# A hybrid decoder layer on one core: the first query block by token, planes and joins by token halves, memory pairs split earlier, and the last root folded into the last sum

## The chip, the core and the metric

One core of a Trainium2 chip runs the whole layer as one program. The metric is the device time of one execution in microseconds. The engines are TensorE (PE, with its weight loads PEld), VectorE (DVE), ScalarE (ACT), GpSimd (POOL) and SyncE (SP). SP issues nearly all DMAs here, the transposing ones too; its queue takes its entries in their order, and so does every engine.

## What is computed

x is 256 tokens by 2048 features, float32. With all weights float32, the reference does

```
hn = rmsnorm(x);  q, k, v, g_ret, xr, yr, g_a, g_b = split(hn @ w_in)
ret_out = silu(g_ret) * groupnorm(retention(rotary(q), rotary(k), v))     # 8 heads
rnn_out = gelu(yr) * rg_lru(causal_dwconv(xr))
h = x + (sigmoid(g_a) * (ret_out @ w_proj_ret) + sigmoid(g_b) * (rnn_out @ w_proj_rnn)) @ w_mix_out
h = h + cross_attention(rmsnorm(h), rmsnorm(mem)) @ xa_w_o                # 256 memory tokens, 4 heads
h = h + (silu(gate) * val) @ ffn_w_down,  gate, val = split(causal_dwconv(rmsnorm(h) @ w_up))
out = rmsnorm(h) * final_norm_w
```

where the last rmsnorm divides each token by sqrt(mean of its 2048 squares + 1e-6).

## The kernel before

**Products.** PE multiplies in a 32-bit format that drops low bits of the operands, so every operand is split into `hi` (rounded) and `lo` (the rest), and each product is done as hi*hi, lo*hi and hi*lo. All products are issued by `mm` (L214) and keep the program's order on PE. A gemm makes a block of 512 output columns for all 256 tokens. `steps_n` makes it by token: the 128 tokens of a half (`tt`) are the stationary operand, 512 weight columns stream, three products per k and half. `steps_t` makes it by feature, for the first query block only: 128 weight columns are stationary and x, hi beside lo, streams; per k four products of 512 columns with the weights' `hi`, and four of 256 with their `lo`. It needs two accumulators; `joined` (L415) adds the two 256-column halves of each (ACT copy L420, DVE sum L421). There are three accumulators in PSUM.

**Weights.** `chunks` and `prefetch` walk through one list of chunks of up to four k (1 MB). For each chunk SP loads `raw` (L252; three buffers), ACT rounds it to `hi` (L279; the very first on DVE, L277) and DVE subtracts for `lo` (L280), two k at a time, with six buffers for each. Loads and splits run two chunks ahead of PE. `later(n, fn)` puts work into the program n + 1 chunks on. The first two blocks, queries and values, alternate chunk by chunk, with sizes 2, 2, 4, 4, 4 (`EARLY`).

**x and mem by feature.** The activations are gathered in `Pairs`: pair i is two k, loaded as `xt` (L533) and split by `split_cols` (ACT L454, DVE L455). A pair is made when it is first asked for; `steps_n` asks ahead after its first token half: for pairs up to min(16, k0 + 3n)/2 - 1.

**Turning blocks.** A block that the next stage needs by feature is turned by DMA: `turned_rows` scales the accumulator into `rows` (DVE, L410 or L412), `by_dma` copies these into two planes of 16-bit halves (`pl`, ACT, L388), two DMA transposes on SP's queue, one for each half of the tokens, turn them into `pt` (L390), and some chunks later `join` puts the planes together as `f` (ACT, L399). The planes are made one word half at a time, over all tokens, and so is the join.

**Residuals.** `residual` makes the four blocks of the mixer's output (and later of the attention's): each is added to the stream on DVE (`nat`, L855), turned by `by_dma`, and split for the next stage's products (`turn`, L454 and L455); `squares` (L873) sums for the norm. `memory_steps` places the memory's work there: the sums from the first block on, and pairs 0 to 3 from the fourth block on, one after each of its chunks. After these blocks come the key and query gemms of the attention (`key_query`); the key gemm reads the memory's pairs.

**The end.** `last_down` makes the last 512 columns in halves of 256 (c) per 128 tokens (tt): add (L1029), sum of squares (L1031), then the sums of all blocks together (L1036, L1037), mean plus eps (`rsqrt_small`, L513), the power -1/2 on POOL (L515), the scaling on DVE and ACT (L1042, L1046, L1048) and the stores (L1050).

**Order.** Instructions are put on each engine by a scheduler with priorities: normally the program's order, earlier under `tc.high_priority`; products and the sums over x are held in order.

Of the kernel before, what the change touches and what calls it, by code (L numbers as in the profile page):

```python
# [17 lines left out]
P = 128  # L18
D = 2048
# [13 lines left out]
PART_BUFS = 6  # L33
AHEAD = 2
WARM = 8
URGENT = 5
FREE = 300
RG_WAIT = 3
EPS = 1e-6
# [99 lines left out]
def hybrid_layer(  # L139
# [38 lines left out]
    def acc():  # L178
        return pm.tile([P, 2, BW], F32, tag="acc", name=nm("acc"))
# [132 lines left out]
            pass  # L312
        return a

    def steps_t(w, row, st, nk, col):

        accs = [acc(), acc()]
        first = gemms[0] == 0
        phase = 0
        for k0, n, parts in chunks(nk, w, row, col):  # L320
            last = k0 + n >= nk
            tiles = [(kk, j) for j in range(2) for kk in range(n)]
            if first and k0 == 0:
                runs = [[(t, pr, kk, j) for t in (0, 1)] for kk in range(n) for pr in range(2) for j in range(2)]
            elif last:
                runs = [[(t, pr, kk, j) for kk, j in tiles] for pr in range(2) for t in (1 - pr, pr)]
            else:
                runs = [[(t, pr, kk, j) for pr in range(2) for kk, j in tiles] for t in (phase, 1 - phase)]
                phase = 1 - phase
            for i, run in enumerate(runs):  # L330
                for t, pr, kk, j in run:
                    k = k0 + kk
                    sx = st[k // 2][:, k % 2, :]
                    part = parts[kk // KH][t][:, kk % KH, (2 * pr + j) * P : (2 * pr + j + 1) * P]
                    a = accs[pr][:, j, :]
                    if t == 1:
                        a, sx = a[:, S:BW], sx[:, 0:S]
                    mm(
                        a, part, sx, start=k == 0 and t == 0, stop=k == nk - 1 and t == 0, skip_group_check=True
                    )  # L340
                if i + 1 == len(runs) // 2 and not last and not first and isinstance(st, Pairs):
                    st[(k0 + n) // 2 + 1]
            yield accs

    def gemm_t(*args):
        return ended(steps_t(*args))

    def products_n(o, sx, hi, lo, tt, start, stop):
        h = sx[:, tt * P : (tt + 1) * P]
        l = sx[:, S + tt * P : S + (tt + 1) * P]  # L350
        mm(o, h, hi, start=start, stop=False)
        mm(o, l, hi, start=False, stop=False)
        mm(o, h, lo, start=False, stop=stop)

    def steps_n(w, row, st, nk, col):

        a = acc()
        for k0, n, parts in chunks(nk, w, row, col):
            for tt in range(2):
                for kk in range(n):  # L360
                    k = k0 + kk
                    hi, lo = (t[:, kk % KH, :] for t in parts[kk // KH])
                    products_n(a[:, tt, :], st[k // 2][:, k % 2, :], hi, lo, tt, k == 0, k == nk - 1)
                if tt == 0 and isinstance(st, Pairs):
                    st[min(NT, k0 + 3 * n) // 2 - 1]
            yield a

    def gemm_n(*args):
# [11 lines left out]
    def by_dma(rows, then, wait=1):  # L380


        planes = big([P, 2, 2, BW], U16, s="pl")
        turned_ = big([P, 2, 4, S], U16, s="pt")
        words = rows.bitcast(U16).rearrange("p t (n h) -> p h t n", h=2)
        with tc.high_priority(FREE):
            for h in range(2):
                act.copy(planes[:, :, h, :], words[:, h])  # L388
        for tt in range(2):
            sp.dma_start_transpose(  # L390
                out=turned_.rearrange("p h f s -> p (h f) s")[:, :, tt * P : (tt + 1) * P],
                in_=planes[:, tt].rearrange("p h n -> p (h n)"),
            )

        def join():
            f = big([P, 4, S], s="f")
            halves_ = f.bitcast(U16).rearrange("p f (s h) -> p h f s", h=2)
            for h in range(2):
                act.copy(halves_[:, h], turned_[:, h])  # L399
            then(f)  # L400

        later(wait, join)

    def turned_rows(a, r, then, wait=1):
# [6 lines left out]
                else:  # L411
                    dve.tensor_scalar_mul(rows[:, tt, :], a[:, tt, :], r[:, tt : tt + 1])  # L412
        by_dma(rows, then, wait)

    def joined(a, s="j"):  # L415

        c = tmp("c")
        o = tmp(s)
        with tc.high_priority(URGENT):
            act.copy(c, a[:, :, S:BW])  # L420
            dve.tensor_tensor(out=o, in0=a[:, :, 0:S], in1=c, op=ALU.add)  # L421
        return o

    def split_pair(src, scale=None):

# [115 lines left out]
            return list.__getitem__(self, i)  # L541

    xs = Pairs(x_t, p_mix, 1)
    q_steps = steps_t("w_in", 0, xs, NT, O_Q)
    v_steps = steps_n("w_in", 0, xs, NT, O_V)
    for _ in EARLY[1:]:
        next(q_steps)
# [35 lines left out]
        dve.scalar_tensor_tensor(out=sin, in0=sin, scalar=sign, in1=rsb, op0=ALU.mult, op1=ALU.mult)  # L583
        dve.tensor_tensor(out=cos, in0=cos, in1=rsb, op=ALU.mult)

    qjoin = [joined(t, "q") for t in next(q_steps)]
    assert next(q_steps, None) is None
    later(0, tables)


# [84 lines left out]
    for g in range(2):  # L675
        dec = big([P, 4, S], s="dec")
        vs, turned = [], ([], [])
        for b, o in enumerate((O_Q, O_K)):
            if g + b:
                def rotate_both(f, o=turned[b]):  # L680
                    o.append(rotated(f[:, 0:2, :]))
                    later(0, lambda: o.append(rotated(f[:, 2:4, :])))

                turned_rows(gemm_n("w_in", 0, xs, NT, o + g * BW), None, rotate_both, 2 - b)
            if b == 1:
                sp.dma_start(
                    out=dec,
                    in_=consts[:, C_DEC + g * 4 * S : C_DEC + (g + 1) * 4 * S].rearrange("p (h s) -> p h s", s=S),
                )
            v = gemm_n("w_in", 0, xs, NT, O_V + g * 1024 + b * BW) if g + b else ended(v_steps)  # L690
            if g + b == 0:
                turned[0].extend(rotated(q) for q in qjoin)
            vs.append(split_rows(v, rs0))
        qr, kr = turned
        gates = []
        for b in range(2):
            a = gemm_n("w_in", 0, xs, NT, O_G + g * 1024 + b * BW)
            t = big([P, 2, BW], s="gate")
            for tt in range(2):
                act.activation(t[:, tt, :], a[:, tt, :], AF.Tanh, scale=half_rs0[:, tt : tt + 1])  # L700
            dve.scalar_tensor_tensor(out=t, in0=t, scalar=1.0, in1=a, op0=ALU.add, op1=ALU.mult)
            gates.append(t)
        retain(g, qr, kr, vs, dec, gates)
# [173 lines left out]
    def memory_steps(b):  # L877
        if b == 0:
            ss = sums()
            for c in range(4):  # L880
                later(c, lambda c=c: sum_squares(mnat[c], ss, c))
            later(4, lambda: rsms.append(rstd_rows(ss)))
        if b == 3:
            ms.load(2)
            for k2 in range(4):
                later(k2, lambda k2=k2: ms[k2])

    h1s = []
    ss1 = residual("w_mix_out", merged, h1s, p_xa, memory_steps)
# [126 lines left out]
            last_down(b0, hid, n, 3)  # L1016

    def last_down(b0, hid, n, b):
        h = hrow[b]
        accs = [acc(), acc()]  # L1020
        parts = [p for _, _, ps in chunks(n, "ffn_w_down", b0 * BW, b * BW) for p in ps]
        for tt in range(2):
            for c in range(2):
                cs = slice(c * S, (c + 1) * S)
                for k in range(n):
                    hi, lo = (t[:, k % KH, cs] for t in parts[k // KH])
                    products_n(accs[c][:, tt, 0:S], hid[k // 2][:, k % 2, :], hi, lo, tt, k == 0, k == n - 1)
                y = h[:, tt, cs]
                dve.tensor_add(y, y, accs[c][:, tt, 0:S])  # L1029
                junk = tp.tile([P, S], F32, tag="tr", bufs=2, name=nm("junk"))  # L1030
                dve.scalar_tensor_tensor(  # L1031
                    out=junk, in0=y, scalar=1.0, in1=y, op0=ALU.mult, op1=ALU.mult,
                    accum_out=ss3[:, tt, b + c : b + c + 1],
                )
            part = sp_.tile([P, 1], F32, tag="pt3", bufs=2, name=nm("pt3"))
            dve.tensor_reduce(out=part, in_=ss3[:, tt, 0:4], axis=AX.X, op=ALU.add)  # L1036
            dve.tensor_scalar(out=part, in0=part, scalar1=1.0 / D, scalar2=EPS, op0=ALU.mult, op1=ALU.add)  # L1037
            r = rsqrt_small(ss3[:, tt, 4:5], 1, 1.0 / D, part)
            for c in (1, 0, 3, 2):
                y = hrow[c][:, tt, :]  # L1040
                if c == 3:
                    dve.scalar_tensor_tensor(  # L1042
                        out=y, in0=y, scalar=r, in1=wfin[1][:, 1, :], op0=ALU.mult, op1=ALU.mult
                    )
                elif c == 1:
                    dve.tensor_scalar_mul(y, y, r)  # L1046
                else:
                    act.mul(y, y, r)  # L1048
# [65 lines left out]
```

## Time and profile before

| what | value |
|---|---|
| runs | 2009.7, 2010.22, 2010.87 us; median 2010.22 |
| the profiled execution | 2008.91 us, its span 2007.1 |
| granted PE clock | 0.999 |
| DMA | 423.02 MB, 211 GB/s over the span |
| PE busy | 1995.5 us of the span |
| last product's end, last store's issue | about 1999.3 and 2002.9 us |

Lines of a timeline read: start, duration, engine and source line, operation, output<-input, shape, how many; in brackets how long the engine was idle before, and what ended that. Lines of a group read: line, engine, operation, shapes, how many | busy us, mean ns of one | idle us before, with what ended it. Lines of the list of waits read: total us, times, longest. Product starts in the trace are modelled, so the pitch between products is the better measure.

### The profile page before, as it was taken

How to read it: one execution, taken by the hardware profiler on the slowest of the kernel's cores; microseconds unless marked ns; L12 is line 12 of the kernel's file. 1: busy time of each engine (PE TensorE's matmuls, PEld its weight loads, DVE VectorE, ACT ScalarE, POOL GpSimd, SP SyncE). 2: the span in 40 equal slices, each digit the busy share in tenths (PEclk: the TensorE clock that was granted, in tenths of full speed). 3: DMA queues.
4: the chain of work that ended last, by engine and by line, in shares of the span. 5: the costliest groups of instructions: out<-in, count | busy, mean ns of one | idle time of the engine just before them, and what ended most of it. 6: DMA issues, size and time to landing. Idle time of an engine off the chain costs nothing.

```text
span 2007.1 us, 23602 instructions
## 1 busy us (share of the span) xinstructions
PE 1995.5 (99%) x9044; PEld 1661.7 (83%) x9044; DVE 1264.2 (63%) x1563; ACT 1248.7 (62%) x1506; POOL 7.7 (0%) x12
## 2 busy tenths in 40 slices
PE   9999999999999999999999999999999999999998
PEld 8888888888888888887888888888888888888887
DVE  6857757888545555457555555666775576664675
ACT  6546648888444455577666655767763566744763
POOL 0000000000000000000000000000000000000000
PEclk9999999999999999999999999999999999999999
DMA  8655657665555566787666545666565566655663
GB/s 318 237 209 168 237 201 197 225 203 186 218 197 191 192 209 212 255 255 249 198 221 213 180 170 195 222 197 232 195 226 210 199 196 219 224 209 201 209 231 126
DMA packets 189376, 423.02 MB, mean 211 GB/s; under 512 B 131664, under 2 KB 136400, under 8 KB 144208
## 3 DMA queue, kind: packets, MB, share of 16 engines
q1 hardware_dynamic: 188832, 421.00, 61.9%
q8 instruction: 70, 1.15, 0.2%
q10 hardware_dynamic: 432, 0.53, 0.1%
q14 instruction: 42, 0.34, 0.0%
HBM read 388.46 MB, written 2.10 MB: 195 GB/s over the span
## 4 chain that ended last, share of the span: by engine, by line
PE 97%; DMA 1%; issue 1%; DVE 0%; ACT 0%; SPq 0%; POOLq 0%; POOL 0%; DVEq 0%; ACTq 0%
PE acc L214 95%; PE sm L214 3%; DMA raw<-in_wall 0%; DMA pt<-pl 0%; DVE lo L280 0%; SPq L252 0%; DVE s L455 0%; SPq L533 0%; ACT f L399 0%; ACT nat L1048 0%; ACT junk L873 0%; DVE nat L855 0%; ACT pl L388 0%; ACT hi L279 0%; POOLq L1110 0%
## 5 line engine op out<-in xcount | busy, mean ns | idle before, releaser
L214 PE MATMUL acc<-hi,s 128*128 128x512 f32 (+1 forms) x5680 | 1739.0, 388 | 1.6 <-DVE s L455 1.6
L280 DVE TENSOR_TENSOR lo<-raw,hi 128x1024 fp32r<-128x1024 f32 (+1 forms) x714 | 860.2, 1219 | 645.5 <-ACT hi L279 628.6
L214 PEld LDWEIGHTS acc<-hi,s 128*128 128x128 f32 x5680 | 1061.7, 188 | 218.9 <-DVE s L455 2.4
L214 PE MATMUL acc<-lo,s 128*128 128x512 f32 (+1 forms) x2840 | 1099.8, 387 | 0.0
L279 ACT CAST hi<-raw 128x1024 fp32r<-128x1024 f32 (+1 forms) x712 | 733.7, 1048 | 500.2 <-PE acc L214 433.7
L214 PEld LDWEIGHTS acc<-lo,s 128*128 128x128 f32 x2840 | 533.2, 188 | 109.1
L399 ACT COPY f<-pt 128x1024 uint16<-128x1024 uint16 x118 | 151.5, 1348 | 76.4 <-DMA pt<-pl 76.4
L388 ACT COPY pl<-rows 128x1024 uint16<-128x1024 uint16 x90 | 89.7, 1044 | 63.8 <-DVE rows L412 55.9
L412 DVE TENSOR_SCALAR rows<-acc,ro 128x512 f32<-128x512 f32 x68 | 47.7, 742 | 3.2 <-PE acc L214 3.2
L971 DVE SCALAR_TENSOR_TENSOR fv<-f,pf,fv 128x255 f32<-128x255 f32 (+1 forms) x88 | 35.8, 477 | 0.7 <-ACT fv L969 0.7
L971 DVE SCALAR_TENSOR_TENSOR fg<-f,pf,fg 128x255 f32<-128x255 f32 (+1 forms) x88 | 35.6, 477 | 0.0
L455 DVE SCALAR_TENSOR_TENSOR s<-f,pb,s 128x256 fp32r<-128x256 f32 x48 | 20.1, 479 | 4.7 <-ACT s L454 4.7
L969 ACT ACTIVATE fv<-f,pf 128x256 f32<-128x256 f32 x44 | 22.8, 590 | 0.0
L969 ACT ACTIVATE fg<-f,pf 128x256 f32<-128x256 f32 x44 | 22.8, 591 | 0.0
L431 ACT ACTIVATE s<-fo 128x512 fp32r<-128x512 f32 x22 | 13.6, 633 | 14.2 <-DVE fo L991 14.2
L780 DVE SCALAR_TENSOR_TENSOR xr<-f,pa,xr 128x255 f32<-128x255 f32 (+2 forms) x48 | 19.9, 478 | 3.2 <-ACT xr L778 3.2
L388 ACT COPY pl<-nat 128x1024 uint16<-128x1024 uint16 x16 | 15.9, 1042 | 8.6 <-DVE nat L855 8.6
L454 ACT ACTIVATE s<-f,pb 128x256 fp32r<-128x256 f32 x48 | 20.6, 498 | 0.0
L214 PEld LDWEIGHTS sm<-s,s 128*128 128x128 f32 x144 | 18.8, 191 | 0.9
L214 PE MATMUL sm<-s,s 128*128 128x256 f32 (+1 forms) x144 | 18.6, 279 | 0.0
L214 PE MATMUL acc<-s,hi 128*128 128x512 f32 x64 | 16.5, 394 | 0.6 <-ACT hi L279 0.4
L443 ACT ACTIVATE v<-acc,ro 128x512 fp32r<-128x512 f32 x16 | 10.9, 684 | 7.7 <-DVE v L444 7.7
(152 smaller groups left out, 623.3 us busy)
## 6 DMA issues: line engine op xcount, KB each, us to landing
raw<-in_wall SPq DMA_DIRECT2D x352, 1024.0 KB, 4.9
nat<-in_x SPq DMA_DIRECT2D x8, 512.0 KB, 8.8
raw<-in_wall SPq DMA_DIRECT2D x6, 512.0 KB, 8.3
nat<-in_mem SPq DMA_DIRECT2D x4, 512.0 KB, 9.3
xt<-in_mem_t SPq DMA_DIRECT2D x8, 256.0 KB, 4.6
pt<-pl SPq DMA_TRANSPOSE x118, 4.3
xt<-in_x_t SPq DMA_DIRECT2D x7, 256.0 KB, 8.4
out<-nat SPq DMA_DIRECT2D x6, 256.0 KB, 2.8
```

Of the source, the lines that this page charges most:

```text
L214: tc.keep_in_program_order(pe.matmul(*a, **k))
L279: act.copy(hi[:, ds], raw[:, cs, :])
L280: dve.tensor_tensor(out=lo[:, ds], in0=raw[:, cs, :], in1=hi[:, ds].bitcast(F32), op=ALU.subtract)
L388: act.copy(planes[:, :, h, :], words[:, h])
L399: act.copy(halves_[:, h], turned_[:, h])
L412: dve.tensor_scalar_mul(rows[:, tt, :], a[:, tt, :], r[:, tt : tt + 1])
L431: act.mul(t[:, :, 0:S], src, scale)
L454: act.activation(t[:, j, 0:S], src[:, j, :], AF.Identity, scale=wcol(j))
L455: dve.scalar_tensor_tensor(out=t[:, j, S:BW], in0=src[:, j, :], scalar=wcol(j), in1=t[:, j, 0:S].bitcast(F32), op0=ALU.mult, op1=ALU.subtract,
L780: dve.scalar_tensor_tensor(out=y[:, s:S], in0=z[:, 0 : S - s], scalar=p_cw(3 - s, t), in1=y[:, s:S], op0=ALU.mult, op1=ALU.add,)
L969: act.activation(y, z[:, j, :], AF.Identity, scale=pf[:, 2, t : t + 1], bias=pf[:, 3, t : t + 1])
L971: dve.scalar_tensor_tensor(out=y[:, s:S], in0=z[:, j, 0 : S - s], scalar=pf[:, 2 - s, t : t + 1], in1=y[:, s:S], op0=ALU.mult, op1=ALU.add,)
```

## The change

`steps_t` and `joined` are gone. The first query block is made by `steps_n`; in its first chunk the products of the two token halves are interleaved so that those with the weights' `lo` come last for each k. The block is turned by `turned_rows` like all others, its join 3 chunks later, and rotated then. `by_dma` makes planes, and joins, one token half at a time. Memory pairs 0 to 3 are placed from the third block's third chunk on. In `last_down` the last block goes to a tile `last` with one more column, which holds sqrt(sum of the other squares + eps * D), made on POOL while the last products run; the last sum of squares takes that column along, with a factor 1/D, and so gives mean plus eps at once.

```diff
-    def steps_t(w, row, st, nk, col):
...
     def products_n(o, sx, hi, lo, tt, start, stop):
         mm(o, h, hi, start=start, stop=False)
         mm(o, l, hi, start=False, stop=False)
+        yield
         mm(o, h, lo, start=False, stop=stop)
+        yield
...
     def steps_n(w, row, st, nk, col):
         a = acc()
+        first = gemms[0] == 0
         for k0, n, parts in chunks(nk, w, row, col):
-            for tt in range(2):
+            if first and k0 == 0:
                 for kk in range(n):
-                    products_n(a[:, tt, :], st[k // 2][:, k % 2, :], hi, lo, tt, k == 0, k == nk - 1)
-                if tt == 0 and isinstance(st, Pairs):
-                    st[min(NT, k0 + 3 * n) // 2 - 1]
+                    for _ in zip(*(tile_(tt, kk) for tt in range(2))):
+                        pass
+            else:
+                for tt in range(2):
+                    for kk in range(n):
+                        for _ in tile_(tt, kk):
+                            pass
+                    if tt == 0 and isinstance(st, Pairs):
+                        st[min(NT, k0 + 3 * n) // 2 - 1]
...
-        words = rows.bitcast(U16).rearrange("p t (n h) -> p h t n", h=2)
-        with tc.high_priority(FREE):
-            for h in range(2):
-                act.copy(planes[:, :, h, :], words[:, h])
+        words = rows.bitcast(U16).rearrange("p t (n h) -> p t h n", h=2)
         for tt in range(2):
+            with tc.high_priority(FREE):
+                act.copy(planes[:, tt], words[:, tt])
             sp.dma_start_transpose(
...
-            for h in range(2):
-                act.copy(halves_[:, h], turned_[:, h])
+            for tt in range(2):
+                cs = slice(tt * P, (tt + 1) * P)
+                act.copy(halves_[:, :, :, cs], turned_[:, :, :, cs])
...
-    def joined(a, s="j"):
...
-    q_steps = steps_t("w_in", 0, xs, NT, O_Q)
+    q_steps = steps_n("w_in", 0, xs, NT, O_Q)
...
-    qjoin = [joined(t, "q") for t in next(q_steps)]
-    assert next(q_steps, None) is None
+    q0 = ended(q_steps)
...
+            a = gemm_n("w_in", 0, xs, NT, o + g * BW) if g + b else q0
+            turned_rows(a, None, rotate_both, 2 - b if g + b else 3)
...
-            if g + b == 0:
-                turned[0].extend(rotated(q) for q in qjoin)
...
-        if b == 3:
+        if b == 2:
             ms.load(2)
             for k2 in range(4):
-                later(k2, lambda k2=k2: ms[k2])
+                later(2 + k2, lambda k2=k2: ms[k2])
...
     def last_down(b0, hid, n, b):
+            last = big([P, BW + 1], s="last")
+                y = last[:, c * S : (c + 1) * S + c]
+                dve.tensor_add(last[:, cs], h[:, tt, cs], accs[c][:, tt, 0:S])
-                    out=junk, in0=y, scalar=1.0, in1=y, op0=ALU.mult, op1=ALU.mult,
+                    out=junk[:, 0 : S + c], in0=y, scalar=1.0 / D if c else 1.0, in1=y, op0=ALU.mult, op1=ALU.mult,
                     accum_out=ss3[:, tt, b + c : b + c + 1],
-            dve.tensor_reduce(out=part, in_=ss3[:, tt, 0:4], axis=AX.X, op=ALU.add)
-            dve.tensor_scalar(out=part, in0=part, scalar1=1.0 / D, scalar2=EPS, op0=ALU.mult, op1=ALU.add)
-            r = rsqrt_small(ss3[:, tt, 4:5], 1, 1.0 / D, part)
+                if c == 0:
+                    dve.tensor_reduce(out=before, in_=ss3[:, tt, 0:4], axis=AX.X, op=ALU.add)
+                    dve.tensor_scalar_add(before, before, EPS * D)
+                    pool.tensor_tensor(out=last[:, BW : BW + 1], in0=before, in1=half, op=ALU.pow)
+            r = sp_.tile([P, 1], F32, tag="ro", bufs=5, name=nm("ro"))
+            pool.tensor_tensor(out=r, in0=ss3[:, tt, 4:5], in1=mhalf[:, 0:1], op=ALU.pow)
```

More of the change, by code (lines that the diff above doesn't have):

```diff
@@ L35 @@
 WARM = 8
-URGENT = 5
 FREE = 300
@@ L313, in ended @@
         return a
-    def steps_t(w, row, st, nk, col):
[L317 to L346, printed above, removed]
     def products_n(o, sx, hi, lo, tt, start, stop):
@@ L352, in products_n, with tile_ @@
         mm(o, l, hi, start=False, stop=False)
+        yield
         mm(o, h, lo, start=False, stop=stop)
+        yield
     def steps_n(w, row, st, nk, col):
         a = acc()
+        first = gemms[0] == 0
         for k0, n, parts in chunks(nk, w, row, col):
-            for tt in range(2):
-                for kk in range(n):
-                    k = k0 + kk
-                    hi, lo = (t[:, kk % KH, :] for t in parts[kk // KH])
-                    products_n(a[:, tt, :], st[k // 2][:, k % 2, :], hi, lo, tt, k == 0, k == nk - 1)
-                if tt == 0 and isinstance(st, Pairs):
-                    st[min(NT, k0 + 3 * n) // 2 - 1]
+            def tile_(tt, kk):
+                k = k0 + kk
+                hi, lo = (t[:, kk % KH, :] for t in parts[kk // KH])
+                return products_n(a[:, tt, :], st[k // 2][:, k % 2, :], hi, lo, tt, k == 0, k == nk - 1)
+            if first and k0 == 0:
+                for kk in range(n):
+                    for _ in zip(*(tile_(tt, kk) for tt in range(2))):
[7 more added lines that the diff above has]
+                        st[min(NT, k0 + 3 * n) // 2 - 1]
             yield a
@@ L413, in turned_rows @@
         by_dma(rows, then, wait)
-    def joined(a, s="j"):
[L417 to L422, printed above, removed]
     def split_pair(src, scale=None):
@@ L678, in hybrid_layer, with rotate_both @@
         for b, o in enumerate((O_Q, O_K)):
[L679 to L684, printed above, removed]
+            def rotate_both(f, o=turned[b]):
+                o.append(rotated(f[:, 0:2, :]))
+                later(0, lambda: o.append(rotated(f[:, 2:4, :])))
+            a = gemm_n("w_in", 0, xs, NT, o + g * BW) if g + b else q0
+            turned_rows(a, None, rotate_both, 2 - b if g + b else 3)
             if b == 1:
@@ L1019, in last_down @@
         h = hrow[b]
+        half = sp_.tile([P, 1], F32, tag="half", bufs=1, name="half")
+        dve.memset(half, 0.5)
         accs = [acc(), acc()]
@@ L1022, in last_down @@
         for tt in range(2):
+            last = big([P, BW + 1], s="last")
+            before = sp_.tile([P, 1], F32, tag="pt3", bufs=2, name=nm("pt3"))
             for c in range(2):
@@ L1026, in last_down @@
                     hi, lo = (t[:, k % KH, cs] for t in parts[k // KH])
[L1027 to L1030, printed above, removed]
+                    for _ in products_n(accs[c][:, tt, 0:S], hid[k // 2][:, k % 2, :], hi, lo, tt, k == 0, k == n - 1):
+                        pass
+                y = last[:, c * S : (c + 1) * S + c]
+                dve.tensor_add(last[:, cs], h[:, tt, cs], accs[c][:, tt, 0:S])
+                junk = tp.tile([P, S + 1], F32, tag="tr", bufs=2, name=nm("junk"))
                 dve.scalar_tensor_tensor(
-                    out=junk, in0=y, scalar=1.0, in1=y, op0=ALU.mult, op1=ALU.mult,
+                    out=junk[:, 0 : S + c], in0=y, scalar=1.0 / D if c else 1.0, in1=y, op0=ALU.mult, op1=ALU.mult,
                     accum_out=ss3[:, tt, b + c : b + c + 1],
                 )
-            part = sp_.tile([P, 1], F32, tag="pt3", bufs=2, name=nm("pt3"))
-            dve.tensor_reduce(out=part, in_=ss3[:, tt, 0:4], axis=AX.X, op=ALU.add)
-            dve.tensor_scalar(out=part, in0=part, scalar1=1.0 / D, scalar2=EPS, op0=ALU.mult, op1=ALU.add)
-            r = rsqrt_small(ss3[:, tt, 4:5], 1, 1.0 / D, part)
+                if c == 0:
[4 more added lines that the diff above has]
+            pool.tensor_tensor(out=r, in0=ss3[:, tt, 4:5], in1=mhalf[:, 0:1], op=ALU.pow)
             for c in (1, 0, 3, 2):
@@ L1042, in last_down @@
                     dve.scalar_tensor_tensor(
-                        out=y, in0=y, scalar=r, in1=wfin[1][:, 1, :], op0=ALU.mult, op1=ALU.mult
+                        out=y, in0=last[:, 0:BW], scalar=r, in1=wfin[1][:, 1, :], op0=ALU.mult, op1=ALU.mult
                     )
```

## The prediction

> **What bounds the kernel now.** I read the busy rows first, then the list of waits with TensorE as the waiter, then the timeline around each of those waits, at the start and at the end.
>
> ```profile
> PE 1995.5 (99%) x9044; PEld 1661.7 (83%) x9044; DVE 1264.2 (63%) x1563; ACT 1248.7 (62%) x1506; POOL 7.7 (0%) x12
> PE acc L214 <- DVE s L455: 1.6, 2, 1.3
> PE warm L211 <- DVE mhalf L206: 1.1, 1, 1.1
> PE acc L214 <- DVE lo L280: 0.5, 2, 0.4
> PE acc L214 <- ACT hi L279: 0.4, 1, 0.4
> PE acc L214 <- DVE hi L277: 0.2, 1, 0.2
> ```
>
> PE is busy 99% of the span, at a granted clock of 0.999. The change removes no product: both forms of the first query block stream 3072 columns for each of 16 k. So a gain can only be PE's waits, the cost of a product's shape, and the tail after the last product. Without the warm-up, which is untouched, the waits sum to 1.6 + 0.5 + 0.4 + 0.2 = 2.7 us. That is a ceiling, and it is small: 0.13% of the time. The two waits of 1.6 us on the splits of L455 are here:
>
> ```profile
> 910.48 1.21 DVE L855 TENSOR_TENSOR nat<-nat,acc 128x1024 f32<-128x1024 f32 x1
> 916.75 1.70 ACT L454 ACTIVATE s<-xt,pb 128x256 fp32r<-128x256 f32 x4
> 918.55 1.67 DVE L455 SCALAR_TENSOR_TENSOR s<-xt,pb,s 128x256 fp32r<-128x256 f32 x4
> 919.08 0.50 PE L214 MATMUL acc<-hi,s 128*128 128x512 f32 x1 [1.27 <-DVE s L455]
> ...
> 1296.02 1.67 DVE L455 SCALAR_TENSOR_TENSOR s<-f,pb,s 128x256 fp32r<-128x256 f32 x4
> 1296.55 0.50 PE L214 MATMUL acc<-hi,s 128*128 128x512 f32 x1 [0.37 <-DVE s L455]
> ```
>
> The pitch of 512-column products is 0.227 us (24 of them from 23.23 to 28.67). By that pitch the first place loses 0.10 us at 917.31 and 1.54 at 919.08, together 1.65; the second loses 0.76 - 0.23 = 0.53 (products at 1295.79 and 1296.55).
>
> **Part 1, first query block by token.** Before, a chunk of four k is 16 products of 512 columns and 16 of 256:
>
> ```profile
> 28.67 3.79 PE L214 MATMUL acc<-s,hi 128*128 128x512 f32 x16
> 32.30 2.08 PE L214 MATMUL acc<-s,lo 128*128 128x256 f32 x16
> 34.21 0.63 PE L214 MATMUL acc<-hi,s 128*128 128x512 f32 x2
> ...
> 11.36 2.11 PE L214 MATMUL acc<-s,hi 128*128 128x512 f32 x8 [0.35 <-ACT hi L279]
> 11.34 1.23 DVE L280 TENSOR_TENSOR lo<-raw,hi 128x1024 fp32r<-128x1024 f32 x1 [0.89 <-ACT hi L279]
> 17.81 1.93 PE L214 MATMUL acc<-s,lo 128*128 128x256 f32 x14 [0.37 <-DVE lo L280]
> ```
>
> It takes 34.21 - 28.67 = 5.54 us; 24 products of 512 take 5.44. That saves 0.10 in each of chunks 3 and 4. Before 23.23 the block goes with its data. In chunk 0 the new order wants `lo` only as its fifth product, which takes away some 0.2 us, but that lead ends at the wait for the weights at 11.36. From there, by token: two products, then a wait until `lo` is there at 11.34 + 1.23 = 12.57 (0.8 us, new); the third product at 12.61 and ten pitches make 14.88; the value chunk of 12 products ends at 17.60; by then `lo` of the next chunk, late at 17.81 before, is nearly done and is wanted only at 19.0 for its second part; 24 products make 23.04, against 23.23. So 0.2 here and 2 x 0.1 later: **-0.4 us**. Ends: +0.4 (the new wait is paid and the old one at 17.81 stays) and -0.7 (both old waits go).
>
> [...]
>
> What the block moves: two L421 sums (0.69 each) and two L420 copies (0.59) go. Two row copies of L410 (0.64), two L388 copies (1.04), two transposes on SP's queue and two L399 copies (1.35) come. DVE's work is unchanged, which matters, as it is busy 4.9 to 5.0 in each 5 us from 45 to 75 us. ACT gets some 3.6 us more; it has 1.6 to 2.4 free in each 5 us from 50 to 65. The turned block is wanted by the scores only, after 140 us, so this costs nothing; without that cover, the 5 us between a block's end and its copies would stand. The loads of x pairs 6 and 7 (512 KB) move ahead of the weights of the fourth value chunk. At some 400 GB/s that is 1.3 us later for these; their `lo` ends at 30.5 and PE wants it at 34.2: 3.7 us of slack, nothing.
>
> **Part 2, planes by token halves.** The same count of copies; the first needs only the first half of the rows.
>
> ```profile
> L399 ACT COPY f<-pt 128x1024 uint16<-128x1024 uint16 x118 | 151.5, 1348 | 76.4 <-DMA pt<-pl 76.4
> L388 ACT COPY pl<-rows 128x1024 uint16<-128x1024 uint16 x90 | 89.7, 1044 | 63.8 <-DVE rows L412 55.9
> 1281.68 2.00 ACT L388 COPY pl<-nat 128x1024 uint16<-128x1024 uint16 x2 [1.18 <-DVE nat L855]
> 1283.70 5.50 SPq L390 DMA_TRANSPOSE pt<-pl  x2
> 1291.38 2.56 ACT L399 COPY f<-pt 128x1024 uint16<-128x1024 uint16 x2 [1.32 <-DMA pt<-pl]
> ```
>
> Before the wait at 1296.55 the chain is copies, transposes at 1283.70, landing, 1291.38, `f`, splits. The first transpose can now go one copy earlier, 0.96 us, and the second follows it; the first join can start when its half is there. A microsecond of gain is more than the 0.53 lost, so that wait goes: **-0.5 us**. What is late next there is `lo` for the same chunk, done at 1296.1. A join copy has the same 1024 elements but runs of 128; no row shows it. Ends: 1044 ns, as the plane copy; 2 x 1348 if short runs halve the rate. I take 1348, the same bytes at the same steps. At 2.7 us two joins add 2.7 to a chain that gains 1.0: the 0.53 becomes 2.2, +1.7. The other turned blocks are off the path, since no other wait of PE is on them.
>
> [...]
>
> **Part 3, memory pairs two chunks (10.9 us) earlier.** The third output block ends near 884.8, the fourth near 906.5 (from the add at 863.00, which waited for PE, plus 96 products each). Yet the fourth's add, L855, runs at 910.48, behind memory splits at 904.14 and 908.55 on DVE. ACT's plane copies, squares and pairs 4 and 5 follow in order, and these are what PE waits for at 917.31 and 919.08. With pairs 0 to 3 split between 879 and 896, where ACT idles 2.08 us and DVE 3.7 and 3.1 us at a time, 1.8 us of ACT and 1.75 us of DVE leave the stretch 904 to 910, the add comes 0.8 to 4 us sooner, and the split 1.65 us late is in time or 0.8 late. I take **-1.5 us** (ends 0 and -1.65), since only the product order, not ACT's, is fixed there. The loads of pairs 6 and 7, at 918.49 behind the transposes, move with them.
>
> **Part 4, the tail.**
>
> ```profile
> 1999.82 0.42 DVE L1031 SCALAR_TENSOR_TENSOR junk<-nat 128x256 f32<-128x256 f32 x1
> 2000.17 0.08 DVE L1031 DVE_READ_ACCUMULATOR junk<-nat 128x1 f32 x1
> 2000.29 0.21 DVE L513 TENSOR_SCALAR rv<-ss,pt 128x1 f32<-128x1 f32 x1
> 2000.58 0.56 POOL L515 TENSOR_TENSOR ro<-rv,mhalf 128x1 f32<-128x1 f32 x1 [7.99 <-DVE rv L513]
> ```
>
> L513 and its gap go; POOL follows the read at 2000.25 by the same 0.08: 2000.33 for 2000.58, **-0.25 us**. L1036 and L1037 were off the path already (1996.0). The new root on POOL (0.56) has the 3.05 us that DVE waits before 1999.36; without them it would cost 0.56. Ends 0 and -0.3.
>
> **Sum.** -0.4 - 1.5 - 0.5 - 0.25 = -2.65 us. The profiled execution took 2008.91 (span 2007.1), so 2006.26; it lies 1.31 under the median 2010.22, so against that median 2007.6.
>
> **Rivals.**
> (a) Likeliest, 0.60: as summed, 2007.6, own range 2006.6 to 2008.6.
> (b) The waits are handed on, 0.20: another split or load on the in-order ACT queue is late in place of pairs 4 and 5, and the new 0.8 us wait at 12.61 is paid (+0.4). For it: DVE waits for ACT in 272 places. Against: only two such waits reach PE. +0.4 + 0 - 0.5 - 0.25 = -0.35: 2009.9.
> (c) Slower, 0.15: the query block's transposes stand in SP's queue ahead of a weight chunk. Place: K's second chunk, whose load went out near 37.8 when its buffer came free; the program lists it behind the transposes. If rows and planes come late on the full DVE (to 50 us) and two transposes take 1.3 us each, it goes out at 52.7, lands 4.9 later at 57.6, and `hi` (1.05) ends at 58.65 against 56.1 wanted; `lo` adds 0.75: 3.3 us. It decides from an issue after some 49.5. Against: at 76.22 a weight load was put ahead of the transposes at 77.12. -2.65 + 3.3 = +0.65: 2010.9; with the next chunk late too, as long again, 2014.2.
> (d) Both old start waits and all others go, 0.05: -0.7 - 1.65 - 0.53 - 0.27 = -3.15: 2007.1, and with the lowest of the spread of runs (1.3 us under) 2005.8.
> That halves are not told apart, so a join waits for both transposes, would leave the earlier first transpose, and the 0.5 us: inside (a).
>
> **Range and chances.** 2005.9 to 2011.2 takes in (a), (b), (d) and the near part of (c). 0.2% is 4.0 us, about what a measurement of this kernel tells from no change; it needs more than all of PE's waits. Faster by that 0.04 (part of d), slower 0.09 (far part of c and dear joins), within 0.87.
>
> **What would show it.** PE's list: no L455 wait near 917 or 1296, one on `lo` of about 0.8 near 11.8, none at 17.8. The add of the fourth block before 910. POOL 0.08 after the accumulator read. Join rows near 1348. I am wrong if a PE wait on `hi` or raw weights appears between 45 and 75 us, or if joins are over 1.9 us (from there the 0.5 is lost).

## The result, and the profile after

The changed kernel takes 2007.07 us (median of 21 executions, 2006.58 to 2007.98); the kernel before took 2009.63 beside it (21 executions, 2008.25 to 2010.87). The ratio is 0.9986 [0.9981, 0.9992], 2.56 us less, which is 0.13%: no change by the bound of 0.2% that the prediction set, but a real one. The granted clock is 0.999 as before. The profiled execution took 2007.17 (span 2005.4; before 2008.91, span 2007.1). The start differs from one execution to the next: the first product stood between 4.62 and 5.45 us in all the traces of this study. So spans are not compared below, but lengths between the starts of two fixed products in the timeline.

In the kernel after, lines have new numbers: the product L213, the splits of weights L276 to L279, those of activations L424 and L425, the planes L367, their transposes L368, the joins L378, the row copies L389, the weight loads L251, the memory loads L503. The list of waits with TensorE as the waiter (us in total, times, longest) is whole here:

```profile
PE warm L210 <- DVE half L990: 1.1, 1, 1.1
PE acc L213 <- DVE hi L276: 0.9, 2, 0.5
PE acc L213 <- DVE lo L279: 0.7, 2, 0.5
```

Both waits on the splits of activations are gone. The waits on L276 belong to the landing of the first loads (products at 5.24 and 7.59): ahead of the first, ACT waits 0.96 us for `pa`, and ahead of the second, DVE waits 0.59 us for `raw`. The timeline of the kernel after, at the place of the big old wait:

```profile
908.00 1.22 DVE L823 TENSOR_TENSOR nat<-nat,acc 128x1024 f32<-128x1024 f32 x1
...
912.39 1.70 ACT L424 ACTIVATE s<-xt,pb 128x256 fp32r<-128x256 f32 x4
914.00 1.99 ACT L278 CAST hi<-raw 128x1024 fp32r<-128x1024 f32 x2
```

The fourth block's add runs 2.5 us sooner (910.48 before), since the splits of memory pairs 0 to 3 no longer stand ahead of it, and the splits of pairs 4 and 5 start at 912.39 for 916.75. Before, ACT did a weight split ahead of these; now it comes after them. From the gate products of the recurrence's last block (479.36; 478.52 before) to the first product of the softmax block (972.44; 973.39), the stretch that holds this place, the trace has 493.08 us for 494.87: 1.79 less.

The turn of the last block of the attention's residual, which the products near 1296 read, in the timeline of the kernel after:

```profile
1281.68 1.23 SPq L368 DMA_TRANSPOSE pt<-pl  x1
1283.01 0.53 SPq L251 DMA_DIRECT2D raw<-in_wall  x1
1283.63 1.23 SPq L368 DMA_TRANSPOSE pt<-pl  x1
1285.64 1.35 ACT L378 COPY f<-pt 128x1024 uint16<-128x1024 uint16 x1
...
1290.18 1.35 ACT L378 COPY f<-pt 128x1024 uint16<-128x1024 uint16 x1 [1.07 <-DMA pt<-pl]
1293.62 1.67 DVE L425 SCALAR_TENSOR_TENSOR s<-f,pb,s 128x256 fp32r<-128x256 f32 x4
```

The first join stands alone, early, and ACT does weight splits between the two; DVE's splits of `f` start at 1293.62 for 1296.02. What nobody asked for: the two transposes of this block no longer stand together. The scheduler put a weight load of 1 MB between them; 26 of the 60 turned blocks are parted now, and none was before. In 44 of the 60 the first join starts before the second transpose has landed; before, it never did. From the last head's product with the values (1199.46; 1200.41 before) to the last add the trace has 798.29 us for 798.95, 0.66 less.

At the start, in the timeline of the kernel after, one wait is as forecast and one is not:

```profile
11.92 1.23 DVE L279 TENSOR_TENSOR lo<-raw,hi 128x1024 fp32r<-128x1024 f32 x1 [0.90 <-ACT hi L278]
13.20 0.50 PE L213 MATMUL acc<-lo,s 128*128 128x512 f32 x1 [0.53 <-DVE lo L279]
...
45.74 1.29 DVE L389 COPY rows<-acc 128x512 f32<-128x512 f32 x2 [4.47 <-PE acc L213]
46.95 1.22 DVE L279 TENSOR_TENSOR lo<-raw,hi 128x1024 fp32r<-128x1024 f32 x1
48.22 0.50 PE L213 MATMUL acc<-lo,s 128*128 128x512 f32 x1 [0.22 <-DVE lo L279]
```

At 13.20 the third product of the second weight chunk waits for `lo`, two products after 11.94: by the pitch some 0.8 us. None is left near 17.8. But near 48 there is a new one. The query block's row copies (L389) have high priority, so the scheduler put them on DVE ahead of a split of weights. They wait 4.47 us for PE to end the block, the split behind them waits too, and then PE waits for that split. The four small products that spread the norm's factor over the tokens (`spread_tokens`, at 45.54; 45.24 before), called the diagonal below, follow the first query and value blocks. From the first of them to the first score product the trace has 98.92 us for 98.38: 0.54 lost.

The tail, in the timeline of the kernel after:

```profile
1997.75 0.42 DVE L1003 TENSOR_TENSOR last<-nat,acc 128x256 f32<-128x256 f32 x1 [3.05 <-PE acc L213]
...
1998.63 0.08 DVE L1005 DVE_READ_ACCUMULATOR junk<-last 128x1 f32 x1
1998.79 0.54 POOL L1014 TENSOR_TENSOR ro<-ss,mhalf 128x1 f32<-128x1 f32 x1 [3.33 <-DVE junk L1005]
```

The power follows 0.08 after the read ends, and 1.04 us after the last add's start; before it was 1.22.

### The profile page after: what moved, and what is told of

It reads as the page before. It is cut to its first block, busy times and chain, and to the rows that moved or that the text cites. A ratio compares the mean times of both kernels' runs of the same rounds, so it can differ in the third digit from the quotient of the medians.

```text
span 2005.4 us, 23496 instructions
## 1 busy us (share of the span) xinstructions
PE 1995.0 (99%) x9012; PEld 1660.5 (83%) x9012; DVE 1264.9 (63%) x1562; ACT 1257.4 (63%) x1508; POOL 8.8 (0%) x14
## 4 chain that ended last, share of the span: by engine, by line
PE 98%; issue 0%; DMA 0%; DVE 0%; SPq 0%; ACT 0%; POOLq 0%; POOL 0%
PE acc L213 96%; PE sm L213 3%; DMA raw<-in_wall 0%; DVE lo L279 0%; SPq L251 0%; ACT nat L1024 0%; DVE rows L389 0%; ACT hi L278 0%; POOLq L1086 0%; POOL last L1012 0%; SPq L503 0%; SPq L253 0%; SPq L500 0%; POOLq L1012 0%
## 5 line engine op out<-in xcount | busy, mean ns | idle before, releaser
L213 PE MATMUL acc<-hi,s 128*128 128x512 f32 (+1 forms) x5744 | 1758.6, 388 | 0.9 <-DVE hi L276 0.9
L213 PEld LDWEIGHTS acc<-hi,s 128*128 128x128 f32 x5744 | 1073.9, 188 | 220.9 <-issue 1.6
L279 DVE TENSOR_TENSOR lo<-raw,hi 128x1024 fp32r<-128x1024 f32 (+1 forms) x714 | 859.7, 1219 | 600.3 <-ACT hi L278 579.9
L213 PE MATMUL acc<-lo,s 128*128 128x512 f32 (+1 forms) x2872 | 1112.1, 387 | 0.7 <-DVE lo L279 0.7
L278 ACT CAST hi<-raw 128x1024 fp32r<-128x1024 f32 (+1 forms) x712 | 733.3, 1048 | 490.7 <-PE acc L213 450.0
L213 PEld LDWEIGHTS acc<-lo,s 128*128 128x128 f32 x2872 | 539.2, 188 | 111.6 <-DVE lo L279 1.6
L378 ACT COPY f<-pt 128x1024 uint16<-128x1024 uint16 x120 | 158.2, 1354 | 94.7 <-DMA pt<-pl 94.7
L367 ACT COPY pl<-rows 128x1024 uint16<-128x1024 uint16 x92 | 91.6, 1043 | 41.8 <-DVE rows L391 37.5
L425 DVE SCALAR_TENSOR_TENSOR s<-f,pb,s 128x256 fp32r<-128x256 f32 x48 | 20.1, 479 | 4.9 <-ACT s L424 4.9
L424 ACT ACTIVATE s<-f,pb 128x256 fp32r<-128x256 f32 x48 | 20.6, 497 | 0.0
L367 ACT COPY pl<-nat 128x1024 uint16<-128x1024 uint16 x16 | 15.9, 1042 | 7.3 <-DVE nat L823 7.3
L213 PEld LDWEIGHTS sm<-s,s 128*128 128x128 f32 x144 | 18.8, 191 | 0.9
L213 PE MATMUL sm<-s,s 128*128 128x256 f32 (+1 forms) x144 | 18.6, 279 | 0.0
L957 ACT ACTIVATE ft<-fg 128x512 f32<-128x512 f32 x22 | 13.8, 629 | 7.3 <-DVE fg L939 7.3
```

What stands on the lines that cost most here:

```text
L213: tc.keep_in_program_order(pe.matmul(*a, **k))
L278: act.copy(hi[:, ds], raw[:, cs, :])
L279: dve.tensor_tensor(out=lo[:, ds], in0=raw[:, cs, :], in1=hi[:, ds].bitcast(F32), op=ALU.subtract)
L367: act.copy(planes[:, tt], words[:, tt])
L378: act.copy(halves_[:, :, :, cs], turned_[:, :, :, cs])
L424: act.activation(t[:, j, 0:S], src[:, j, :], AF.Identity, scale=wcol(j))
```

## The experiments

The kernel before was run beside each set. Its medians there were 2009.56, 2009.52 and 2009.73, and 2009.63 above, so a difference of medians under some 0.2 to 0.3 us is not told apart here. "Against the change" below is the difference of a variant's median to 2007.07.

**no_mem: the change with the memory pairs where they were.**

```diff
-        if b == 2:
+        if b == 3:
             ms.load(2)
             for k2 in range(4):
-                later(2 + k2, lambda k2=k2: ms[k2])
+                later(k2, lambda k2=k2: ms[k2])
```

> The changed kernel with the memory pairs 0 to 3 placed as before, from the fourth output block on. Theory (each part takes away its own wait of TensorE): the two waits at the key gemm's third chunk come back, near 917, and cost 1.65 us: about 2008.7 where the changed kernel has 2007.1. Rival (the earlier planes and transposes are enough to have pairs 4 and 5 in time): no wait there, no difference beyond 0.3 us.

Measured: 2010.64 (2009.54 to 2011.4, 11 executions), ratio 1.0002 [0.9993, 1.0011]: 3.57 against the change, twice what any theory had, and all of the change's gain. The profiled execution is the slowest of the eleven (2011.4). The timeline of no_mem:

```profile
918.45 0.51 SPq L251 DMA_DIRECT2D raw<-in_wall  x1
...
920.34 1.10 SPq L503 DMA_DIRECT2D xt<-in_mem_t  x2
...
926.72 1.71 ACT L424 ACTIVATE s<-xt,pb 128x256 fp32r<-128x256 f32 x4 [2.06 <-DMA xt<-in_mem_t]
927.28 1.02 PE L213 MATMUL acc<-hi,s 128*128 128x512 f32 x2 [1.30 <-ACT s L424]
```

A 1 MB weight load has slipped between the transposes of 917.11 and 919.05, so it now stands ahead of the last two memory loads. The first of these lands 6.35 us after its issue; before, issued at 918.49, it took 3.51. Another stands at 894.32, ahead of the first six. ACT waits for memory, and PE for ACT. The stretch from the gate to the softmax block takes 496.30, 3.22 more than in the change and 1.43 more than before. So in this execution the other parts of the change make the old place of the memory pairs dearer than it was.

**no_halves: the change with planes and joins by word halves, as before.**

```diff
-        words = rows.bitcast(U16).rearrange("p t (n h) -> p t h n", h=2)
+        words = rows.bitcast(U16).rearrange("p t (n h) -> p h t n", h=2)
+        with tc.high_priority(FREE):
+            for h in range(2):
+                act.copy(planes[:, :, h, :], words[:, h])
...
-            with tc.high_priority(FREE):
-                act.copy(planes[:, tt], words[:, tt])
...
-            for tt in range(2):
-                cs = slice(tt * P, (tt + 1) * P)
-                act.copy(halves_[:, :, :, cs], turned_[:, :, :, cs])
+            for h in range(2):
+                act.copy(halves_[:, h], turned_[:, h])
```

> The changed kernel with planes and joins by word halves as before. Theory: the wait before the first feed-forward block's last chunk, near 1296, comes back and costs 0.5 us, nothing else moves: about 2007.6 against 2007.1. Rival (the earlier start of the run moves that chunk's data too, so the wait was going anyway, or other blocks gained by halves): 0, or over 1 us with waits at other blocks.

Measured: 2008.41 (2007.31 to 2011.11, 11 executions), ratio 0.9996 [0.9988, 1.0005]: 1.34 against the change, and three of the executions over 2010.5. One of these was profiled (2010.79). Its timeline:

```profile
1471.90 2.57 ACT L378 COPY f<-pt 128x1024 uint16<-128x1024 uint16 x2 [5.09 <-DMA pt<-pl]
...
1475.40 1.23 DVE L279 TENSOR_TENSOR lo<-raw,hi 128x1024 fp32r<-128x1024 f32 x1 [6.96 <-ACT hi L278]
...
1484.52 0.50 PE L213 MATMUL acc<-lo,s 128*128 128x512 f32 x1 [0.68 <-DVE lo L279]
```

ACT stands 5.09 us at a pair of joins, the weight split behind them comes late, DVE waits 6.96 us for it, works without a pause from then on, and PE waits for `lo`. PE's waits on `lo` are 1.7 us in four places: here, at 1501.39, and twice at the start, as in the change. The forecast wait near 1296 is not in this execution. Against the change, 2.04 us are lost from the last head to the last add, and 1.26 from the gate to the softmax block, at the key gemm (918.97 to 925.12). ACT stands until both transposes have landed, and the time of a pair in SP's queue differs from one execution to the next (6.04 us for 5.50 in before_again, below); that this makes the spread of 3.8 us was not shown, since one execution was profiled.

**no_token: the change with the first query block transposed by products, as before** (`steps_t` and `joined` put back; the edit is the first part of the diff, reversed).

> The changed kernel with the first query block by feature and joined by ACT and DVE as before. The prediction's step says 0.4 us slower than the changed kernel. The changed kernel's trace says otherwise: a wait of some 0.5 us on the weights' lo near 48 us, put behind the row copies on DVE, eats the gain of 0.26 to 0.34 us before it; by this the run is 0.2 to 0.3 us faster than the changed kernel, and its trace has no wait of TensorE near 48.

Measured: 2007.08 (2006.42 to 2007.37, 11 executions), ratio 0.9987 [0.9978, 0.9995]: 0.0 against the change. There is no wait near 48 in it, and that on `lo` at 17.97 is back. Neither the prediction's 0.4 nor the 0.2 to 0.3 the other way came out: the token form brings nothing in sum that these runs can tell.

**no_tail: the change with `last_down` as before**, but for the loop over the products' generator.

> The changed kernel with the end as before (sums added, mean plus eps, then the root). The prediction's step says 0.25 us slower than the changed kernel; the two traces, from the last add to GpSimd's power, say 0.18 (1.04 against 1.22). Rival: nothing, if the stores end by another chain.

Measured: 2007.31 (2006.75 to 2007.72, 11 executions), ratio 0.9989 [0.998, 0.9997]: 0.24 against the change, at the edge of what the medians tell apart; from add to power 1.22 us, as before.

**calm: the query block's row copies at ordinary priority**, so that DVE may do weight splits while PE ends the block.

```diff
-    def turned_rows(a, r, then, wait=1):
+    def turned_rows(a, r, then, wait=1, ahead_=FREE):
...
-        with tc.high_priority(FREE):
+        with tc.high_priority(ahead_):
...
-            turned_rows(a, None, rotate_both, 2 - b if g + b else 3)
+            turned_rows(a, None, rotate_both, 2 - b if g + b else 3, FREE if g + b else 0)
```

> The changed kernel with the first query block's two row copies at ordinary priority, which lets the weights' lo of the fifth value chunk stand ahead of them on DVE. Theory (the wait near 48 is made by the row copies that wait for TensorE ahead of that lo): the wait goes, 0.5 us faster than the changed kernel, about 2006.6. Rival (that lo is late for its load or its hi): the wait stays, no difference.

Measured: 2006.70 (2006.28 to 2007.5, 11 executions), ratio 0.9987 [0.9978, 0.9996]: -0.37 against the change. The wait near 48 is gone and the stretch behind the diagonal takes 98.40 us, for 98.92. So the wait came from the row copies' place on DVE.

**two_chunks: the second weight chunk by token in turn too**, so that `lo` is wanted later.

```diff
-            if first and k0 == 0:
+            if first and k0 < 4:
```

> The changed kernel with the interleaved order of products in the query block's second chunk too, where TensorE waits 0.8 us for lo after two products. With both token halves interleaved per k, four products (0.9 us) lie ahead of that lo. Theory: 0.4 to 0.5 us of the 0.8 goes: about 2006.6. Rival (the data that follow are late anyway, so the time is only moved): no difference, and a wait on lo some us later.

Measured: 2006.75 (2006.11 to 2007.57, 11 executions), ratio 0.9987 [0.9978, 0.9996]: -0.32 against the change. The wait at 13.20 is gone; that near 48 is there still (0.2, at 47.56).

**both: calm and two_chunks together.**

> The changed kernel with both of the edits tried alone beside it: interleaving in the second chunk, and row copies of the first query block at ordinary priority. Theory: the two add up, 0.9 to 1.0 us faster than the changed kernel, about 2006.1. Rival: either gain is lost at the data that follow, 0 to 0.5 us.

Measured: 2006.14 (2005.5 to 2007.12, 11 executions), ratio 0.9982 [0.9973, 0.9991]: -0.93 against the change, and the fastest kernel here. Only the waits on the warm-up and on L276 are left to PE (1.1 and 0.9 us).

**only_mem: the kernel before with the memory pairs moved** (the edit of no_mem, reversed, on the kernel before).

> The kernel before with the memory pairs 0 to 3 two chunks earlier, and nothing else changed. Theory: the waits at 917 go, 1.5 to 1.65 us faster than before, about 2008.0; the wait near 1296 stays. Rival (the halves are needed for it too): less than 0.8 us faster, with a smaller wait left near 917.

Measured: 2008.76 (2006.68 to 2010.24, 11 executions), ratio 0.9996 [0.9987, 1.0004]: 0.76 less than before beside it (2009.52), half of the 1.5 to 1.65 expected, and not clear of no difference. Its trace has the whole gain at the old place: 493.08 us from the gate to the softmax block, 1.79 less than before. The wait near 1296 stays and is longer (0.75 in the list for 0.37): the stretch to the last add takes 0.56 more than before. The executions scatter over 3.6 us, the change's over 1.4; what scatters in the others is not seen, since one was profiled.

**only_halves: the kernel before with planes and joins by token halves** (the edit of no_halves, reversed, on the kernel before).

> The kernel before with planes and joins by token halves alone. Theory (from the run without the memory's move): the scheduler now puts a weight load of 1 MB between the two transposes, ahead of the memory loads that follow them, which so land later than before and make TensorE wait in the key gemm: 0.8 to 1.4 us slower than before, about 2010.7. Rival (the prediction's: the halves only bring turned blocks forward): 0.5 us faster than before, 2009.0.

Measured: 2009.45 (2008.55 to 2012.05, 11 executions), ratio 0.9997 [0.9988, 1.0006]: 0.28 less than before beside it (2009.73), which decides for neither theory. Its profiled execution is its slowest. There the wait near 1296 is gone (798.29 us from the last head to the last add, as in the change), and the wait for memory is larger: 497.20 us from the gate to the softmax block, 2.33 over before. So in this execution the halves give in one place and take in the other while memory stands where it was.

**planes_only and joins_only: one half of the second part each.** The first has planes and transposes by token and joins by word; the second planes by word and joins by token.

```diff
# planes_only, against the change
-            for tt in range(2):
-                cs = slice(tt * P, (tt + 1) * P)
-                act.copy(halves_[:, :, :, cs], turned_[:, :, :, cs])
+            for h in range(2):
+                act.copy(halves_[:, h], turned_[:, h])
# joins_only, against the change
+        with tc.high_priority(FREE):
+            for h in range(2):
+                act.copy(planes[:, :, h, :], words[:, h])
...
-            with tc.high_priority(FREE):
-                act.copy(planes[:, tt], words[:, tt])
```

> The changed kernel with planes by token halves but joins by word halves. If the gain of halves is in the transposes (issued one copy earlier, and a weight load between them in place of SP standing), this stays within 0.3 us of the changed kernel, 2007.1 to 2007.4. If it is in the first join's start on the first half, it loses most of 1.3 us: 2008.4.

> The changed kernel with planes by word halves, so that both transposes wait for both copies and stand together, and joins by token halves. If the gain of halves is in the transposes, this is like the kernel with neither, 2008.4; if in the joins, like the changed kernel, 2007.1.

Measured: planes_only 2016.99 (2016.26 to 2017.25, 5 executions), ratio 1.0036 [1.0024, 1.0049]: 9.9 us slower than the change. joins_only 2007.25 (2006.88 to 2007.58, 11 executions), ratio 0.9986 [0.9977, 0.9995]: as the change (+0.18). By joins_only the gain lies in the joins. planes_only is neither of the two values on record (2007.1 to 2007.4, or 2008.4): that it would be 8.6 us slower than with neither half, no theory had. The timeline of planes_only:

```profile
1417.48 1.23 SPq L368 DMA_TRANSPOSE pt<-pl  x1
1418.80 0.53 SPq L251 DMA_DIRECT2D raw<-in_wall  x1
1419.42 1.23 SPq L368 DMA_TRANSPOSE pt<-pl  x1
...
1426.04 2.55 ACT L377 COPY f<-pt 128x1024 uint16<-128x1024 uint16 x2 [5.74 <-DMA pt<-pl]
1429.54 1.23 DVE L279 TENSOR_TENSOR lo<-raw,hi 128x1024 fp32r<-128x1024 f32 x1 [7.79 <-ACT hi L278]
...
1436.31 0.50 PE L213 MATMUL acc<-lo,s 128*128 128x512 f32 x1 [0.82 <-DVE lo L279]
```

The second transpose stands behind the weight load. A join by word halves needs both transposes, so ACT stands 5.74 us; the weight splits behind it come late on ACT, then on DVE, and PE waits. PE's waits on `lo` are 7.2 us in seven places, two of them at the start, as in the change. The load between is not all of it. At this block the joins of no_halves start at 1426.04 too, and PE does not wait there: ACT has done one more weight split (L278, 1420.17) ahead of them. At the block of 1282.98 both halves have landed 8.2 us after the first issue, for 6.4 in no_halves. How the 9.9 us divide between later landings and ACT's order was not tested.

In the change the same load stands between the transposes (1283.01), but the first join does not wait for it. In joins_only the transposes stand together, as one row of two (1282.73, 4.24 us). The first half lands at 1288.21 and its join starts at 1288.23, 0.8 before the second half lands; the splits of `f` are in time. In joins_only the first join starts before the second landing in 45 of 60 blocks, in planes_only and no_halves in none.

**before_again: the kernel before, profiled once more**, to see which waits are the same in two executions.

> The kernel before, unchanged, for a second trace of it. If the waits near 917 and 1296 are of one size in each execution, they are 1.65 and 0.53 us again within 0.2 us. If they come from the landing of transposes and loads, which the runs of this kernel over a span of 4 us suggest, one of them differs by more than 0.5 us.

Measured: 2009.49 (one execution), span 2007.7. From the gate to the softmax block 494.78 us (494.87 in the first profile): the wait for memory is the same. From the last head to the last add 799.52 (798.95): the wait near 1296 is 0.57 longer. The transposes ahead of it took SP's queue 6.04 us for 5.50, and the joins start at 1291.96 for 1291.38. PE's waits on L455 are 2.0 us in all, for 1.6.

## Why the prediction was right, and where its steps were not

The sum was -2.65 us, and -2.56 came out. The median that the prediction stood on (2010.22, three executions) was 0.6 above that of 21; without that, 2006.98 would have stood against 2007.07. No change by 0.2% and rival (a) held, and so did the ceiling of 2.7, for this change. The terms held less well than their sum. By the lengths in the two traces they are -1.79 for memory, -0.66 for the halves, +0.26 for the query block and -0.18 for the tail, -2.37 in all: 0.45 more gain than forecast in the first two, and 0.66 less in the third. That the sum came so near is in part luck.

As a ceiling on what can be gained, 2.7 is too low: `both` is 3.38 under the kernel before beside it, of which the shape (0.25) and the tail (0.18) are no waits. The list counts a wait from the end of the last product, and it is these ends, not the starts, that are modelled: at 919.08 it has 1.27, where the pitch between starts gives 1.54.

- **Memory pairs, -1.5 forecast.** Right in place and cause by the trace, and nearly in size: 1.79, a little beyond the far end of -1.65, with the add at 908.00. Of the order on ACT, left open there, it turned out that pairs 4 and 5 now come ahead of the weight split. But its worth hangs on the rest: 0.76 by medians if made alone, which is not clear of nothing, and 3.57 if taken out of the change.
- **Halves, -0.5 forecast.** The wait of 0.53 went, but for half of the reason given. "The first transpose can now go one copy earlier" brings nothing that the medians tell apart (joins_only), and costs 9.9 us if the joins stay as they were (planes_only), where a weight load goes between the transposes and a weight split less goes ahead of the joins; the prediction saw neither. "The first join can start when its half is there" is the gain. The part taken out whole costs 1.34: mis-sized in "The other turned blocks are off the path", since only one wait of one execution was counted, and in the profiled execution of no_halves the time is lost at other blocks. The joins took 1354 ns, with 1348 chosen: the two forms of the join are 6 ns apart in these traces. Why the plane copies take 1043 in the same trace is not shown.
- **Query block by token, -0.4 forecast, 0.0 measured.** Three sizes were off. From 11.36 to 23.23, 11.87 us before, the working had 0.2 less; it is 11.94 to 23.78, 11.84: nothing. Of what is missing, 0.11 is the product behind the wait (13.20 to 13.54, where the working took the pitch). From there to the diagonal it is 21.76 for 22.01, 0.25 less, with 0.2 forecast. And the new wait near 48 takes 0.54 back. That step failed in "DVE's work is unchanged": its work was, its order was not. Rival (c) looked for a late weight chunk at this place, through SP's queue and with a price of 3.3; it came through DVE's and cost a sixth of that. The sign of being wrong named `hi` and raw weights between 45 and 75 us; the wait that came there was on `lo`.
- **Tail, -0.25 forecast.** 0.18 by the trace, 0.24 by the medians, which hardly tell that much apart. L513 and its gap are gone, but the last squares start 0.53 after the add's start, where it was 0.46; the trace names no cause.

Rival (b), waits handed on, was true of the small wait near 48 and not of the rest. Rival (d) did not come: PE still waits for `lo` at 13.20 and at 48.22.

Open: the four parts taken out one by one make 3.57 + 1.34 + 0.24 + 0.0 = 5.15, twice the whole gain, so they lean on each other. That the slipped weight load is what makes no_mem so slow is read from its queue and its waits; no kernel with the joins by token, the transposes together and memory late was run. What the scheduler does to ACT's order when the joins are halved was not parted from their start on one half. That the scatter of no_halves and only_mem comes from joins was not shown.

## What to carry to other kernels

A copy that waits for a transfer held up the work behind it on its engine here (in no_halves ACT stood 5.09 us at a pair of joins, and DVE 6.96 us for the weight split behind them), so cut such a copy to what one transfer brings. When a pair of transfers is cut in two, look at what the scheduler puts between them, and who needs both (planes_only was 9.9 us slower than the change). And a copy of high priority that waits for PE belongs in the sum with all the work that it is put ahead of, even where the engine's total work is unchanged (here it waited 4.47 us, and the stretch lost 0.54).

## What was not expected of the hardware

A DMA transpose that does not stand beside another in SP's queue mostly took that queue 1.23 to 1.26 us (49 of 52 in the change, the others up to 2.30); two that stand together took 2.60 (at 870.02 in the change), 4.24 (joins_only), 5.50 (before, at 1283.70) and 6.87 (no_halves, at 1417.11). The median from issue to landing was 3.3 us after and 4.3 before; from a block's first issue to its last landing it was 5.6 and 6.0. What makes the pair so uneven is not shown.

The spread of equal executions changed with the change, 1.4 us for 2.6 (21 executions each); it was 3.8 in no_halves, and 0.7 in joins_only (11 each).
